# A chunked recurrence cut into pieces: hand-placed half steps with a fixed order on each engine, in place of a scheduler's order

## The chip, the cores and the metric

The kernel runs on one core of a Trainium2 chip. The metric is the device time of one execution in microseconds (us); three runs of the kernel before have a median of 3324.03 us (3309.18 to 3331.33). Names: PE is TensorE, DVE VectorE, ACT ScalarE, POOL GpSimd, SP SyncE, on whose queue the transfers stand.

## What is computed

Three layers of a transformer-like model run one after another in one launch. The change touches the middle one, whose mixer is a recurrence over 256 context positions and 512 positions of the sequence, for 16 heads of 64 channels, once forwards and once backwards:

```python
def step(S, inp):                       # S: 64 x 64 state of one head
    w_t, k_t, v_t, kk_t, kka_t = inp[:5]
    S = (S * w_t[:, :, None, :]
         - jnp.einsum('bhij,bhj->bhi', S, kk_t)[..., None] * kka_t[:, :, None, :]
         + v_t[..., None] * k_t[:, :, None, :])
    y = jnp.einsum('bhij,bhj->bhi', S, inp[5]) if emit else None
    return S, y
...
for d, reverse in enumerate((False, True)):
    s_ctx, y_c = wkv_scan(s0, decay_c, k_dc, v_c, kk_c, a_c, r_c, reverse)
    _, y_d = wkv_scan(s_ctx, decay, k_d, v, kk, a, r, reverse)
    ys.append(y_d)
y = rwkv_readout(ys[0] + ys[1], r, ..., v, g, r_k, ln_g, ln_b, wo, h.dtype)
```

The readout normalises y by head, adds a bonus (the sum over r, k and a weight, times v), multiplies by the gate g and by the matrix wo.

## The kernel before

The recurrence (`class Scan`) works on eight blocks of two heads, 128 channels on the partitions. A block holds both directions, and each direction is cut into 12 chunks of 64 positions (4 of context, 8 of the sequence), so that 24 chunk matrices belong to a block.

`front(blk)` makes what a block needs before its recurrence. It loads keys, decays and rates; for each direction it takes a running sum of the decays on VectorE (L328), exponentials on ScalarE (L330, L331), an affine map (L335), and products on VectorE: `ta` (L337), the key product (L340), the bonus product (L342) and the two parts of `bk` (L344, L345). Then come, for each group g of four chunks, the Gram matrices on TensorE (L362), a mask on VectorE (L365), transposes of `bk` on TensorE (L373), and copies on ScalarE into `tw` (L375) and into `Ld` (L379), which holds the 32x32 blocks on the diagonals.

`rest()` solves and runs the block. The triangular solve transposes `Ld` into `M` (L406, VectorE), does 30 steps of two operations each on GpSimd (L411 multiplies, L412 adds; each step depends on the one before), and transposes back twice on VectorE (L416, L417). The fold puts the solved 32x32 blocks together to 64x64 matrices `T` and multiplies them into the Gram parts: copies L421, matmuls L429 and L438 with copies L433 and L441, matmuls L451 with copies L453 (`FX`). The chain is the sequential part, 12 steps:

- TensorE makes `u` from V and the state Z (L467, L485), ScalarE copies it to X (L488);
- TensorE makes `z` (L473, L492, L495), VectorE scales it to the next Z (L498);
- TensorE adds to Y (L503, L504).

The readout follows: squares, sums by head, a reciprocal root on VectorE of nine tiny operations (L595 to L599), a broadcast (L607, L611), the product of v and bonus on GpSimd (L523), and three operations on VectorE (L525, L526, L530).

The program calls `front` and `rest` block by block. Which instruction of one block goes ahead of which of another, on each engine, is decided by a scheduler that orders the traced program ahead of time; each engine then takes its own row strictly in order. `front` of a block may overlap `rest` of the block before it, as two sets of tiles (`hp`) exist. In the last block 192 instructions of the output matmul (L1270) are tied to steps of the chain by `interleave`. PSUM has three buffers of tag `a` (Gram parts, transposes), one each of `f`, `z` and `y`, and two of `u`.

Of the kernel before, what the change touches and what calls it, by code (L numbers as in the profile page):

```python
# [10 lines left out]
F32 = mybir.dt.float32  # L11
# [13 lines left out]
CH = 64  # L25
# [200 lines left out]

class Scan:

# [3 lines left out]
    def __init__(self, prog):  # L232
# [6 lines left out]
        self.fp = self.pool("sc_f", 1, "right")  # L239
# [5 lines left out]
        self.P, self.Ld = {}, {}  # L245
# [41 lines left out]
    def interleave(self, work, steps, first=0):  # L287

        for k, i in enumerate(work):
            g = steps[first + k * (len(steps) - first) // len(work)]  # L290
            self.p.tc.add_manual_dep(i, g.name, mybir.DependencyInfo(mybir.DependencyClass.NoSync, mybir.DependencyReason.DATA), reason="interleave")
# [9 lines left out]
    def front(self, blk):  # L301
# [16 lines left out]
        order = (lambda t: ((slice(0, NT), t),),
                 lambda t: ((slice(0, NC_), t[:, NC_ - 1::-1]), (slice(NC_, NT), t[:, :NC_ - 1:-1])))

        brk = hp.tile([128, 128], F32, name="brk")
        nc.gpsimd.tensor_scalar(brk, self.bdiag, self.p.col("rk", blk), None, ALU.mult)
        bon = self.p.pt("a")
        TW, A = [], []
        for d in range(2):
            s, ta = load("sg", NT, self.p.sd[blk, d]), load("ta", NT, self.p.td[blk, d])
            cs = fp.tile([128, NT], F32, name="cs", tag="cs")
            nc.vector.tensor_tensor_scan(cs, self.mreset, s, 0.0, ALU.mult, ALU.add)  # L328

# [24 lines left out]
            tw = [hp.tile([128, 8 if i else 4, 2, 3 if i else 2, CH], F32, name=f"tw{d}{i}") for i in range(2)]
            side = lambda h, c: bk[dr[h], c, h:h + 2, :].rearrange("p a t -> p (a t)")
            for g in range(3):
                na, t = (2, tw[1][:, g * 4 - 4:g * 4]) if g else (1, tw[0])
                pss = [self.p.pt("a")[:, :4 * na * CH].rearrange("p (c a t) -> p c a t", c=4, a=na) for h in range(2)]
                for c in range(4):
                    for h in range(2):  # L360
                        rhs = al[dr[h], (g - 1) * 4 + c] if g else ac[dr[h], c]
                        nc.tensor.matmul(pss[h][:, c], side(h, g * 4 + c), rhs.rearrange("p a t -> p (a t)"), start=True, stop=True)  # L362
                for h in range(2):
                    mask = self.mscan.rearrange("p (a t) -> p a t", a=2)[:, :na].unsqueeze(1).to_broadcast([128, 4, na, CH])
                    nc.vector.tensor_tensor(t[:, :, h, :na, :], pss[h], mask, ALU.mult)  # L365
                if g == 1:
                    continue

                n, c0 = (8, 4) if g else (4, 0)
                pts = [self.p.pt("a") for h in range(2)]  # L370
                for c in range(n):
# [1551 lines left out]
```

## Time and profile before

| | |
|---|---|
| median of the three runs | 3324.03 us |
| profiled execution: time, span | 3327.71, 3325.9 us |
| mean granted TensorE clock | 0.884 of full speed |
| busy share of the span: PE, DVE, ACT, POOL | 87%, 49%, 44%, 32% |
| first `M` transpose (L406) to last | 1323.1 to 1987.7 us |
| last Y matmul of the recurrence (L504) starts | 2133.7 us |

The recurrence lies between about 1390 and 2134 us of the span. Busy shares are means over the whole program; what lies in the stretch of the recurrence is read from windows and timelines of it alone. The granted clock of TensorE is given as a share of 2.4 GHz, so 0.50 is 1.2 GHz.

### The profile page before, as it was taken

The page shows a single profiled execution, that of the slowest core. Times are in us where ns is not written, and L with a number is a line of the kernel's source. Part 1 is how long each engine was busy: PE and PEld are TensorE (multiplying, and loading weights), DVE is VectorE, ACT ScalarE, POOL GpSimd, SP SyncE. Part 2 cuts the span into 40 slices and gives each one's busy share as a digit, 9 for nine tenths or more (in the row PEclk, how much of TensorE's full clock was granted, in tenths as well). Part 3 has the DMA queues.
Part 4 walks back from the last instruction along what each step waited for, and adds up shares of the span by engine and source line. Part 5 has one row for each costly group of instructions (what it writes and reads, how often), then busy time and mean ns, then how long its engine had stood idle before and what let it go on. Part 6 is the DMA issues. An engine that isn't in the chain of part 4 may idle for free.

```text
span 3325.9 us, 53211 instructions
## 1 busy us (share of the span) xinstructions
PE 2894.5 (87%) x21242; PEld 2431.2 (73%) x21242; DVE 1627.1 (49%) x3063; ACT 1471.5 (44%) x2849; POOL 1054.1 (32%) x1437
## 2 busy tenths in 40 slices
PE   6998989999996999867667765879999799999999
PEld 6966878888884888656556654667778596578887
DVE  7566364444458446342343431164444575555354
ACT  3257566666655534323333331255553435534342
POOL 4014545677654000343333223025551320020000
PEclk9989989999997899866666667889999896999999
DMA  5423223333313523411112112225542121022322
GB/s 213 139 72 101 93 73 115 124 127 125 126 55 130 193 107 133 120 54 25 39 46 52 52 25 84 83 68 178 174 166 100 57 79 45 1 76 85 105 92 87
DMA packets 125048, 317.55 MB, mean 95 GB/s; under 512 B 36480, under 2 KB 44416, under 8 KB 107776
## 3 DMA queue, kind: packets, MB, share of 16 engines
q1 hardware_dynamic: 124800, 314.15, 28.0%
q8 instruction: 167, 2.74, 0.3%
q14 instruction: 81, 0.66, 0.1%
HBM read 275.57 MB, written 38.54 MB: 94 GB/s over the span
## 4 chain that ended last, share of the span: by engine, by line
PE 30%; POOL 8%; ACT 5%; DMA 4%; DVE 4%; issue 2%; SPq 0%; POOLq 0%; ACTq 0%; DVEq 0%
PE mm L574 6%; PE mm L575 6%; PE mm L576 6%; DMA adaw<-in_ada_dram 3%; POOL acc L717 3%; POOL M L412 2%; POOL Mt L411 2%; PE a L362 2%; ACT wh L567 1%; PE a L1270 1%; PE st L1231 1%; ACT adat L716 1%; PE a L1890 1%; PE b L1225 1%; PE a L1893 1%
## 5 line engine op out<-in xcount | busy, mean ns | idle before, releaser
L717 POOL TENSOR_TENSOR acc<-acc,adat 128x256 f32<-128x256 f32 x658 | 575.4, 896 | 543.2 <-ACT acc L713 436.9
L568 DVE TENSOR_TENSOR wl<-wr,wh 128x2048 fp32r<-128x2048 f32 (+3 forms) x145 | 314.6, 2169 | 382.6 <-ACT wh L567 374.8
L716 ACT ACTIVATE adat<-adaw,silu 128x256 f32<-128x256 f32 x644 | 319.8, 508 | 265.0 <-POOL acc L717 169.5
L567 ACT CAST wh<-wr 128x2048 fp32r<-128x2048 f32 (+2 forms) x147 | 264.8, 1801 | 239.8 <-PE mm L575 217.2
L574 PE MATMUL mm<-fh,wh 128*128 128x512 f32 (+1 forms) x1008 | 349.3, 354 | 19.3 <-DVE relu L999 13.2
L575 PE MATMUL mm<-fl,wh 128*128 128x512 f32 (+1 forms) x1008 | 351.8, 351 | 2.6 <-DVE fl L581 2.6
L576 PE MATMUL mm<-fh,wl 128*128 128x512 f32 (+1 forms) x1008 | 351.0, 350 | 1.0 <-DVE wl L568 1.0
L574 PE MATMUL mm<-h_xhi,wh 128*128 128x512 f32 (+1 forms) x784 | 277.6, 359 | 2.7 <-ACT h_xhi L580 2.7
L575 PE MATMUL mm<-h_xlo,wh 128*128 128x512 f32 (+1 forms) x784 | 277.5, 357 | 0.3 <-DVE h_xlo L581 0.3
L576 PE MATMUL mm<-h_xhi,wl 128*128 128x512 f32 (+1 forms) x784 | 277.5, 356 | 0.0
L574 PEld LDWEIGHTS mm<-fh,wh 128*128 128x128 f32 x1008 | 191.0, 190 | 48.2 <-DVE relu L999 15.6
L648 POOL TENSOR_TENSOR acc<-acc,t 128x256 f32<-128x256 f32 x127 | 108.7, 863 | 350.7 <-ACT t L646 347.9
L575 PEld LDWEIGHTS mm<-fl,wh 128*128 128x128 f32 x1008 | 191.6, 190 | 29.1 <-DVE fl L581 5.7
L576 PEld LDWEIGHTS mm<-fh,wl 128*128 128x128 f32 x1008 | 191.3, 190 | 25.8 <-DVE wl L568 1.2
L411 POOL TENSOR_TENSOR Mt<-M 128x30 f32<-128x30 f32 (+14 forms) x240 | 116.9, 487 | 240.2 <-DVE M L406 133.4
L1023 DVE TENSOR_TENSOR y<-mm,y 128x512 f32<-128x512 f32 (+1 forms) x184 | 99.2, 559 | 143.4 <-PE mm L576 142.7
L574 PE MATMUL mm<-h_hi,wh 128*128 128x512 f32 (+1 forms) x408 | 160.7, 398 | 7.2 <-ACT h_hi L669 7.2
L576 PEld LDWEIGHTS mm<-h_xhi,wl 128*128 128x128 f32 x784 | 148.7, 190 | 21.3 <-issue 0.2
L574 PEld LDWEIGHTS mm<-h_xhi,wh 128*128 128x128 f32 x784 | 147.5, 190 | 22.3 <-ACT h_xhi L580 3.0
L575 PEld LDWEIGHTS mm<-h_xlo,wh 128*128 128x128 f32 x784 | 148.7, 191 | 19.3 <-DVE h_xlo L581 0.7
L575 PE MATMUL mm<-h_lo,wh 128*128 128x512 f32 (+1 forms) x408 | 159.9, 393 | 0.0
L473 PE MATMUL z<-V,tw 64*64 64x64 f32 x704 | 46.2, 254 | 130.3 <-DVE Z L498 128.0
(450 smaller groups left out, 7048.0 us busy)
## 6 DMA issues: line engine op xcount, KB each, us to landing
adaw<-in_ada_dram SPq DMA_DIRECT2D x256, 256.0 KB, 2.7
wr<-in_w_dram SPq DMA_DIRECT2D x64, 1024.0 KB, 4.9
wr<-in_wup_dram SPq DMA_DIRECT2D x22, 1024.0 KB, 4.8
wr<-in_wdn_dram SPq DMA_DIRECT2D x16, 704.0 KB, 4.0
wr<-in_win_dram SPq DMA_DIRECT2D x9, 1024.0 KB, 4.9
wr<-in_evin_dram SPq DMA_DIRECT2D x8, 1024.0 KB, 4.8
sd<-lr_out SPq DMA_DIRECT2D x16, 384.0 KB, 2.6
td<-lr_out SPq DMA_DIRECT2D x16, 384.0 KB, 2.3
```

The costliest lines, as they stand in the source:

```text
L362: nc.tensor.matmul(pss[h][:, c], side(h, g * 4 + c), rhs.rearrange("p a t -> p (a t)"), start=True, stop=True)
L411: nc.gpsimd.tensor_tensor(t, a, b, ALU.mult)
L412: nc.gpsimd.tensor_tensor(M[:, s + 1:, :s], M[:, s + 1:, :s], t, ALU.add)
L567: nc.scalar.copy(hi[:, :n], raw[:, :n])
L568: (eng or nc.vector).tensor_tensor(lo[:, :n], raw[:, :n], hi[:, :n], ALU.subtract)
L574: mm(out, lhs[0], rhs[0], start=first, stop=False)
L575: mm(out, lhs[0], rhs[1], start=False, stop=False)
L576: return mm(out, lhs[1], rhs[0], start=False, stop=last)
L648: nc.gpsimd.tensor_tensor(acc, acc, sq, ALU.add)
L716: nc.scalar.activation(t, w, AF.Copy, scale=s)
L717: nc.gpsimd.tensor_tensor(acc, acc, t, ALU.add)
L1023: nc.vector.tensor_tensor(yb, ps[:, :n], yb, ALU.add)
```

## The change

`front` and `rest` are cut into lists of pieces: `elements` (loads, and for each direction decay, keys and bonus), `grams` (six pieces, one for each direction and group), `solve` (five: first transpose; steps 1 to 10 on VectorE; 11 to 20 on GpSimd; 21 to 30 on VectorE; back-transposes), `fold` (11 pieces), `values` (loads of V by group) and `readout` (three). `chain` becomes a generator that stops after each half step, so 24 times. `slot(blk)` walks the chain of one block and issues, behind the half steps named in its tables, the end of the fold of the same block, the solve and fold of the next block, the elements and Gram pieces of the one after, and the readout of the one before. `pin` then ties each instruction on TensorE, VectorE, ScalarE and GpSimd to the one traced before it on the same engine, so that the traced order stands; SP's queue is not tied. `interleave` is gone: the output matmuls are 32 parts of three at half steps 2 to 23 of the last slot.

The key product and the bonus product move from VectorE to GpSimd; 20 of 30 solve steps move from GpSimd to VectorE. The decay tile P is kept once for each direction rather than for each parity, with a small copy PC of its chunk ends; `al` and `tw` are tiles by group, with a third set for the last group; some element tiles have two sets; V has one set of tiles by group. Loads of the output matrix can start when the chain of block 6 ends.

```diff
+    def solve(self, blk):
...
+                eng.tensor_tensor(t, a, c, ALU.mult)
+                eng.tensor_tensor(M[:, s + 1:, :s], M[:, s + 1:, :s], t, ALU.add)
...
-                nc.vector.tensor_tensor(f[:, c], f[:, c], v3(t), ALU.mult)
+                    nc.gpsimd.tensor_tensor(f[:, c], f[:, c], v3(t), ALU.mult)
...
-            nc.vector.tensor_tensor(v3(pr), v3(r if d == 0 else r[:, ::-1]), f[:, NPC:], ALU.mult)
+                nc.gpsimd.tensor_tensor(v3(pr), v3(r if d == 0 else r[:, ::-1]), f[:, NPC:], ALU.mult)
...
+            if p + 1 < NP:
+                U = begin(p + 1)
+            yield
...
+    def slot(self, blk, work=()):
...
+        put(self.fold(blk)[9:], (0, 1))
+        if blk + 1 < 8:
+            put(self.solve(blk + 1), (0, 1, 2, 9, 10))
+            put(self.fold(blk + 1)[:9], (11, 12, 13, 14, 15, 16, 19, 20, 23))
+            put([lambda: self.values(blk + 1, 0), lambda: self.values(blk + 1, 1)], (8, 16))
+        if blk:
+            put([lambda: self.values(blk, 2)], (0,))
+        if blk > 0:
+            put(self.readout(blk - 1), (3, 5, 6))
+        if blk + 2 < 8:
+            put(self.elements(blk + 2), (0, 2, 4, 8, 7, 10, 12))
+            put(self.grams(blk + 2), (13, 14, 17, 18, 21, 22))
...
+        for k, _ in enumerate(self.chain(blk)):
+            for f in at.pop(k, ()):
+                f()
...
-        scan.rest()
-        for blk in range(1, 7):
-            scan.front(blk)
-            scan.rest()
-        scan.front(7)
...
+        for f in scan.elements(1) + fold[:9] + scan.grams(1):
+            f()
+        for blk in range(7):
+            scan.slot(blk)
```

VectorE's row in a block in the middle, before: from the transpose that opens the solve to the first operation of the next block (Z is the chain's state, P the decays, Dd and Ld the solved blocks, ac a Gram operand).

```order
L406 STREAM_TRANSPOSE M<-Ld_13843 128x1024
L498 TENSOR_TENSOR Z<-z,P_12755 128x128 x7
L416 STREAM_TRANSPOSE Ld_13843<-M 128x32x32
L417 STREAM_TRANSPOSE Dd<-M 128x32x32
L498 TENSOR_TENSOR Z<-z,P_12755 128x128 x4
L351 SCALAR_TENSOR_TENSOR ac_17072<-kkin,P_12755 128x256
```

Seven of a block's eleven Z operations stand ahead of the back-transposes, which need the end of the block's own solve, and four behind.

VectorE's row in a slot in the middle, now, with the lines of the changed kernel: from the end of the ten solve steps behind Z0 (L457, L458) over the elements (scan L357, ta L365, bk L376, the copy L366) to Z2 (the three L584) and the first of the readout's nine tiny operations (L621, L732 and on).

```order
L457 TENSOR_TENSOR Mt<-M 128x210
L458 TENSOR_TENSOR M<-M,Mt 128x21x10
L357 SCALAR_TENSOR_TENSOR cs<-mreset,sg 128x768
L365 SCALAR_TENSOR_TENSOR ta<-ta,kkin 128x768
L366 COPY PC<-P_12755 128x12
L584 TENSOR_TENSOR Z<-z,PC 128x128
L621 TENSOR_SCALAR gnv<-f 128x8
L376 TENSOR_TENSOR bk<-ta,cs 128x12x64
L584 TENSOR_TENSOR Z<-z,PC 128x128
L732 TENSOR_SCALAR rs_r<-gnv 128x8
```

A little further in the same row the readout's end stands ahead of Z3, and the second direction's elements ahead of Z4.

```order
L744 COPY rb<-rs_r 128x512
L633 SCALAR_TENSOR_TENSOR ysb<-ysb,cols,f 128x512
L634 SCALAR_TENSOR_TENSOR ysb<-ysb,cols,sq 128x512
L635 TENSOR_TENSOR ysb<-ysb,rb 128x512
L584 TENSOR_TENSOR Z<-z,PC 128x128
L357 SCALAR_TENSOR_TENSOR cs<-mreset,sg 128x768
L365 SCALAR_TENSOR_TENSOR ta<-ta,kkin 128x256
L365 SCALAR_TENSOR_TENSOR ta<-ta,kkin 128x512
L366 COPY PC<-P_12757 128x12
L386 TENSOR_TENSOR bk<-bk,cs 128x12x64
L584 TENSOR_TENSOR Z<-z,PC 128x128
```

The Z operations, which stood alone before, now have solve steps, elements and readout between them, at fixed places.

GpSimd's row in the same slot, now: the last of the ten solve steps, then the readout's product (L623, which writes the sq that L634 above reads), then the key and bonus products (L375, L380).

```order
L457 TENSOR_TENSOR Mt<-M 128x220
L458 TENSOR_TENSOR M<-M,Mt 128x11x20
L623 TENSOR_TENSOR sq<-sq,vb 128x512
L375 TENSOR_TENSOR bk<-bk,kin 128x12x64
L380 TENSOR_TENSOR prod<-rin,bk 128x512
L375 TENSOR_TENSOR bk<-bk,kin 128x4x64
L375 TENSOR_TENSOR bk<-bk,kin 128x8x64
L380 TENSOR_TENSOR prod<-rin,bk 128x512
```

Before, this row held all 60 solve operations of a block in one run and no key or bonus products.

TensorE's row at a pair of Gram pieces, now (L427 Gram matrices and L435 transposes of two pieces; L559, L570, L574, L553 the chain's half step between them; L582 the next one).

```order
L427 MATMUL a<-al,bk 128x128 x8
L435 MATMUL a<-cst,bk 128x64 x8
L559 MATMUL z<-V,tw 64x64 x4
L570 MATMUL u<-Z,al 64x64 x4
L574 MATMUL z<-Z,cst 128x128
L553 MATMUL u<-V,tw 64x64 x4
L427 MATMUL a<-al,bk 128x128 x8
L435 MATMUL a<-cst,bk 128x64 x8
L582 MATMUL z<-X,FX 64x64 x4
```

Before, Gram pieces and fold matmuls stood together with no step of a chain between them; one such float matmul of the order is two instructions of the trace.

## Rows read from the trace of the kernel before

**Rows 1.** Windows: start and end, length, busy us (instructions) of PE, PEld, DVE, ACT, POOL; clock.

```profile
1670.00:1764.00 94.00, 62.25 (x1002) 54.13 (x1002) 35.06 (x60) 29.96 (x64) 32.05 (x63) 0.65 0.18 46
```

**Rows 2.** Instructions of line L406: durations in ns, minimum, median, maximum; first and last start.

```profile
L406 DVE STREAM_TRANSPOSE M<-Ld x8: 1935/1974/2067, 1323.1 to 1987.7; 128x1024 f32<-128x1024 f32 x8
```

**Rows 3.** Timeline of DVE: start, duration (us), instruction, count, idle before and its releaser.

```profile
1721.66 0.29 DVE L498 TENSOR_TENSOR Z<-z,P 128x128 f32<-128x128 f32 x1 [1.62 <-PE z L495]
1741.30 1.91 DVE L416 STREAM_TRANSPOSE Ld<-M 128x1024 f32<-128x1024 f32 x1 [19.35 <-POOL M L412]
```

**Rows 4.** Windows of 3 us in the stage of Gram matrices and fold.

```profile
1679.00:1682.00 3.00, 2.77 (x15) 2.55 (x16) 1.17 (x3) 1.22 (x4) 0.32 (x1) 0.50 0.28 107
...
1682.00:1685.00 3.00, 3.00 (x23) 3.00 (x21) 3.00 (x5) 0.33 (x1) 0.00 (x0) 0.50 0.36 93
...
1703.00:1706.00 3.00, 3.00 (x46) 2.47 (x42) 1.89 (x2) 2.56 (x7) 0.00 (x0) 0.59 0.00 0
1706.00:1709.00 3.00, 2.60 (x48) 1.99 (x48) 0.82 (x2) 1.17 (x3) 1.83 (x7) 1.00 0.41 131
```

**Rows 5.** Timeline of POOL, the solve's steps 1, 11 and 21.

```profile
1706.70 0.25 POOL L411 TENSOR_TENSOR Mt<-M 128x30 f32<-128x30 f32 x1 [27.39 <-PE a L343]
...
1717.13 0.59 POOL L411 TENSOR_TENSOR Mt<-M 128x220 f32<-128x220 f32 x1
...
1731.20 0.55 POOL L411 TENSOR_TENSOR Mt<-M 128x210 f32<-128x210 f32 x1
```

**Rows 6.** Timelines of DVE and POOL where both work.

```profile
1452.93 1.37 DVE L345 TENSOR_TENSOR bk<-bk,cs 128x768 f32<-128x768 f32 x1
...
1452.19 1.29 POOL L411 TENSOR_TENSOR Mt<-M 128x240 f32<-128x240 f32 x1
...
1771.63 0.17 DVE L599 SCALAR_TENSOR_TENSOR rs_r<-rs_t,rs_r 128x8 f32<-128x8 f32 x1
1771.83 1.24 DVE L597 SCALAR_TENSOR_TENSOR rs_t<-rs_r 128x8 f32<-128x8 f32 x1
```

**Rows 7.** Groups by form, 1389.8 to 2135 us: count, busy us, mean ns, idle before.

```profile
L365 DVE TENSOR_TENSOR tw<-a,c_mscan 128x512 f32<-128x512 f32 x56 | 37.2, 686 | 42.1 <-PE a L362 41.9
L328 DVE TENSOR_TENSOR_SCAN cs<-mreset,sg 128x768 f32<-128x768 bf16 x13 | 22.8, 1755 | 11.1 <-DMA sg<-sd 11.1
L379 ACT COPY Ld<-tw 32x128 f32<-32x128 f32 x56 | 16.5, 294 | 25.1 <-DVE tw L365 23.9
L344 DVE TENSOR_TENSOR bk<-ta,cs 128x768 f32<-128x768 f32 x13 | 12.4, 954 | 2.7 <-ACT cs L331 2.7
L335 ACT ACTIVATE bk<-ta,be,al 128x768 f32<-128x768 f32 x12 | 12.3, 1027 | 16.2 <-DMA ta<-td 16.1
L330 ACT ACTIVATE P<-cs 128x768 f32<-128x768 f32 x13 | 10.9, 838 | 17.0 <-DVE cs L328 9.7 <-DVE Z L498 7.4
L375 ACT COPY tw<-a 128x256 f32<-128x256 f32 x28 | 10.0, 373 | 7.0 <-PE a L373 5.9 <-PE a L362 0.3
L523 POOL TENSOR_TENSOR sq<-sq,vb 128x512 f32<-128x512 f32 x7 | 10.0, 1422 | 183.8 <-DMA ta<-td 61.6 <-DMA sq<-vd 56.3 <-issue 34.8
```

**Rows 8.** Timeline of PE at 1.2 GHz: Gram, fold and transposes.

```profile
1681.62 3.74 PE L362 MATMUL a<-al,bk 64*128 64x128 f32 x23
...
1693.48 1.49 PE L429 MATMUL f<-Dd,tw 32*32 32x32 f32 x48
1694.90 0.69 PE L373 MATMUL a<-cst,bk 64*128 64x64 f32 x8
...
1702.45 1.97 PE L451 MATMUL f<-tw,T 64*64 64x64 f32 x32
```

**Rows 9.** Timeline of ACT: the last copy of the values.

```profile
1387.66 0.59 ACT L1525 COPY vblk<-v 128x512 f32<-128x512 f32 x1 [1.82 <-PE v L1522]
```

**Rows 10.** Timeline of DVE in the last block's chain.

```profile
2097.30 0.29 DVE L498 TENSOR_TENSOR Z<-z,P 128x128 f32<-128x128 f32 x1 [5.72 <-PE z L495]
```

**Rows 11.** Instructions of line L504 on PE, columns as in rows 2.

```profile
L504 PE MATMUL y<-FX,X x512: 217/218/366, 1437.6 to 2133.7; 64*64 64x64 f32 x171
```

**Rows 12.** DMA issues of the page: count, KB each, us to landing.

```profile
sd<-lr_out SPq DMA_DIRECT2D x16, 384.0 KB, 2.6
```

More of the change, by code (lines that the diff above doesn't have):

```diff
@@ L243, in __init__ @@
         nc.vector.memset(self.mreset[:, ::CH], 0.0)
-        self.P, self.Ld = {}, {}
+        self.P = []
+        for d in range(2):
+            P = self.cp.tile([128, NT // CH, 1 + CH], F32, name=f"P{d}")
+            nc.vector.memset(P[:, :, 0:1], 1.0)
+            self.P.append(P)
+        self.Ld = {}
         self.fixed(0)
@@ L285, in late, with pin @@
             nc.gpsimd.memset(self.T[q * 32:q * 32 + 32, :, 32:64], 0.0)
[L287 to L291, printed above, removed]
+        cur = nc.cur_bb
+        self.mark = len(cur.bb.instructions)
+    def pin(self):
+        traced = self.nc.cur_bb.bb.instructions
+        last = {}
+        for i in traced[self.mark:]:
+            if str(i.engine) not in PINNED:
+                continue
+            if i.engine in last:
+                self.p.tc.add_manual_dep(i, last[i.engine], mybir.DependencyInfo(mybir.DependencyClass.NoSync, mybir.DependencyReason.DATA),
+                                         reason="order")
+            last[i.engine] = i.name
     def drop(self, q):
@@ L365, in front @@
[L365 to L371, printed above, removed]
+                    mask = self.mscan.rearrange("p (a t) -> p a t", a=2)[:, :na[g]].unsqueeze(1).to_broadcast([128, 4, na[g], CH])
+                    nc.vector.tensor_tensor(tw[:, :, h, :na[g], :], pss[h], mask, ALU.mult)
@@ L509, in rest, with finish @@
+    def finish(self, blk):
+        b = self.B[blk]
+        y = b["y"] = self.tmp.tile([128, NX], F32, name="ysb", tag="ysb", bufs=1)
+        self.nc.scalar.copy(y, b["Y"])
         if blk == 0:
             self.p.tap("ysum0", y)
[L511 to L515 removed]
@@ new lines, in slot, with put @@
+    def slot(self, blk, work=()):
+        at = {}
+        def put(pieces, places):
+            for f, k in zip(pieces, places, strict=True):
+                at.setdefault(k, []).append(f)
+        put(self.fold(blk)[9:], (0, 1))
[10 more added lines that the diff above has]
+            put(self.grams(blk + 2), (13, 14, 17, 18, 21, 22))
+        for k, f in work:
+            at.setdefault(k, []).append(f)
+        for k, _ in enumerate(self.chain(blk)):
+            for f in at.pop(k, ()):
+                f()
+        assert not at
+        self.finish(blk)
@@ L1246, in layer1 @@
         scan.late()
-        scan.rest()
-        for blk in range(1, 7):
-            scan.front(blk)
-            scan.rest()
-        scan.front(7)
-        scan.drop(scan.fp)
+        fold = scan.fold(0)
+        for g in range(3):
+            scan.values(0, g)
+        for f in scan.elements(1) + fold[:9] + scan.grams(1):
+            f()
+        for blk in range(7):
+            scan.slot(blk)
+        scan.drop(scan.fp[0])
         scan.drop(scan.hp[0])
@@ L1536, in features @@
         scan = Scan(self)
-        scan.front(0)
+        for f in scan.elements(0) + scan.grams(0) + scan.solve(0):
+            f()
         values(wv)
```

402 lines of the change are left out of this document (234 added, 168 removed).

## The prediction

> **What bounds the kernel now.** I read the windows by block first, then the timelines of VectorE and GpSimd inside one block, then the TensorE clock in short windows, then the groups by form for prices.
>
> In the block from 1670 to 1764 us no engine is full: TensorE 62 of 94 us at a mean granted clock of 0.65, VectorE 35, ScalarE 30, GpSimd 32 [rows 1]. The eight transposes that open the triangular solve start from 1323.1 to 1987.7 [rows 2]: (1987.7-1323.1)/7 = 94.9 us a block. So a block is bound by waits, and there are two.
>
> First, the chain. A step at 2.4 GHz takes 1.62 us of waiting plus 0.29 = 1.91 us [rows 3]. Seven steps run beside GpSimd's solve; then VectorE's row has the back-transpose (L416) ahead of the eighth Z, and VectorE sits idle 19.35 us until GpSimd ends the solve [rows 3]. From the end of the last Z (1721.66+0.29) to the end of the two transposes (1741.30+1.91, and another such) the chain stands still for some 23 us.
>
> Second, the stage after it, where the next block's Gram matrices and the fold follow each other on TensorE. There the granted clock is 0.50 (1.2 GHz) with TensorE full, from the window at 1679 on, and 2.4 GHz is back only in the window at 1706 [rows 4].
>
> **The change part by part.** Nearly all arithmetic stays; the order decides. I follow one slot from its Z0 to the next slot's Z0 along the in-order rows of the engines.
>
> *What is removed.* No Z stands behind a back-transpose of the block that is about to be folded: the solve is now a block ahead. That frees the 23 us. What takes their place must be walked.
>
> *Z0 to Z3.* Behind Z0 VectorE has ten solve steps, 20 small dependent operations, which the trace has only on GpSimd: there they take 1717.13-1706.70 = 10.4 us [rows 5], the upper bound. The lower one is the 0.20 us from start to start of two tiny dependent operations [rows 6], 20x0.20 = 4.0. With sizes around that of the Z operation (128 columns, 0.29 us [rows 3]) plus a gap I take 6.5. Then GpSimd does steps 11 to 20: 1731.20-1717.13 = 14.1 us [rows 5]. Behind them on its row stands the readout's product with vb, 1.42 [rows 7]; VectorE's L634 (a line of the changed kernel, the second operation of the readout's end) waits for that product, and L635 and Z3 are queued behind L634, and TensorE's next step behind Z3. L634 and L635 cost about 0.69 each (128x512, as L365 [rows 7]), Z 0.29: 6.5+14.1+1.4+1.4+0.3 = 23.7. So the wait for GpSimd comes back, shorter, through the readout.
>
> To this comes what VectorE holds up. Where VectorE's two-input operations met solve operations, they took turns: L345 took 1.37 where L344, of the same size, takes 0.95, and the solve operation beside it 1.29 where another of nearly its size takes 0.59 [rows 5 to 7]. In the 14 us VectorE runs the scan, 1.76, ta and bk, 0.95 each [rows 7], and the readout's nine small ones, some 1 us: 4.7. With it 28.4. Bounds: 4.0+14.1+1.4+1.7 = 21.2 (GpSimd loses nothing) and 10.4+14.1+4.7+1.4+1.7 = 32.3.
>
> The Trainium skill, page "SBUF — State Buffer", section "SBUF: two separate sides", goes further: a VectorE instruction with two SBUF inputs and a GpSimd one that reads SBUF exclude each other for a whole instruction. By that rule each of the nine small operations would wait for a solve operation, and a block would be some 4.5 us longer than by the row. The trace agrees for the long operations and for one tiny one, 1.24 us [rows 6].
>
> *Z3 to Z4.* The second direction's elements: scan 1.76, two exponentials 0.84 each and the affine 1.03 on ScalarE, then ta and bk on VectorE, 0.95 each, Z 0.29 [rows 3, 7]: 6.7. The key products moved to GpSimd: it shows 1.42 at 128x512 [rows 7], so 2.1 at 768 columns; VectorE's 0.95 is the lower bound. They come before bk and take turns with VectorE's own; I take 8 (6.7 to 9.3).
>
> *Z4 to Z5.* The last ten solve steps on VectorE, sizes mirrored, 6.5 again (4.0 to 10.4), two back-transposes of 1.91 [rows 3], bk 0.95, Z 0.29, a small memset: 11.7. With GpSimd's key products beside them 12 (9.2 to 15.6).
>
> *Z5 to Z6.* One step, and bk behind its GpSimd product: 4 (3 to 5). Z0 to Z6 together 28.4+8+12+4 = 52.4. TensorE has little to do in it.
>
> *Z6 to the next Z0.* Three pairs of Gram pieces, one piece at a half step. A piece at 1.2 GHz is 16 instructions at 3.74/23 = 0.163 (2.6 us) and 16 of the transposes at 0.69/8 (1.38) [rows 8]. Tag a has three buffers, so transposes wait for the mask (0.69 [rows 7]), the second piece for the first copy (0.37), and the next Z stands behind both pieces; al costs 0.84 (two operations of 256 columns), z and Z 0.8: 0.84+2x(2.6+0.69+1.38)+0.37+0.8 = 11.3, plus the second piece's copies ahead of the next X (2x0.37+4x0.294 = 1.9 [rows 7]) = 13.2. At 2.4 GHz the matmuls halve: 9.2. Two chain steps without Grams 7.6 or 3.8. Fold: four pieces of 1.49 and five of 1.97 [rows 8], 15.8, or 7.9. In all 63.0 at 1.2 GHz and 39.3 at 2.4. Before, a full TensorE got its clock back after 1706-1679 = 27 us [rows 4]; with 25 us slow, 25/63.0 = 0.40 of the work is done, and the rest fast makes 25+0.60x39.3 = 48.6; I take 50.
>
> So a slot is T = 52.4+50 = 102.4 us against 94.9.
>
> *Ends.* The blocks' values end at 1387.66+0.59 [rows 9]; only then do the pools for elements(1) exist. Per direction scan, three ScalarE operations, three VectorE ones and the key products are about 10 us, 20 for both; 4 of the fold not hidden beside them; three Gram pairs 40 at the slow clock: Z0 of slot 0 at 1388+20+4+40 = 1452. Slot 0 lacks a readout, 8 us less. Slot 6 has no elements and Grams: 23.7+2+11+3 up to Z6 and 26 for five steps and the fold = 66. Slot 7 keeps the output matmuls: twelve steps at 5.72+0.29 = 6.0 [rows 10] and 2 to start: 74. The last Y comes at 1452-8+66+74+6T = 1584+6T = 2198. Before it starts at 2133.7 [rows 11], so 2134, and all behind it is unchanged: +64 us. On the profiled execution's own 3327.7 (span 3325.9) that is 3392; it lies 3.7 above the median shown, so by the median 3388. I say 3390. The sign turns at T = (2134-1584)/6 = 91.7.
>
> Costed at nothing: PC's copies of 12 columns (0.17 as the tiny operations [rows 6], twice a slot), brk on GpSimd (ahead of a whole slot), and the loads: V in groups and the elements' are issued half a slot or more ahead of their readers; without that cover each would show its 2.6 us [rows 12].
>
> **The rivals.** *Warm TensorE* (the other side): the chain steps and fold pieces between the Gram pieces keep the clock at 2.4 GHz from Z6 on. For it: the clock is 1.00 in the window at 1706, where chain and fold mix and TensorE is not even full. Against: the windows before it stayed at 0.50 with TensorE full [rows 4], and Z0 to Z6 leaves TensorE mostly idle. The stage is then 39.3 us, or 2x(1.3+0.69)+1.9 = 5.9 a pair and 29.4 in all if masks and copies hide as well: T = 82 to 92, last Y 2075 to 2134, 3265 to 3324. It decides from a stage of 39.3 us downwards.
>
> *Free port.* VectorE's operations don't hold GpSimd, and its solve steps run at their lower bound: T = 102.4-4.7-2x2.5 = 92.7, 3330, as before. Against it the turns of rows 6.
>
> *Cold TensorE.* The stage is at 1.2 GHz throughout: T = 52.4+63.0 = 115.4, +142, 3466. For it the 27 full microseconds at 0.50 [rows 4].
>
> *Full exclusion.* Each of the nine small operations waits for a solve operation, as one did: 9x0.5 = 4.5 us more, T = 106.9, +91, 3415. Against it: the one before it took 0.17 [rows 6]. The Trainium skill's page "SBUF — State Buffer" has this as its rule.
>
> That the change doesn't do what it says (a Z still behind the transposes that wait for GpSimd's whole solve) the order excludes; only its price is open.
>
> **How the numbers follow.** My forecast, T from 95 to 109: 0.38, 3345 to 3430. Warm TensorE 0.30, two thirds of it under 3291. Free port 0.10. Warm and free together 0.05 (T about 77, 3236). Cold 0.10. Full exclusion 0.07. A difference under 1% (33 us) can't be told from none here. Faster by over 1%: 0.20+0.05 = 0.25. Within 1% (3291 to 3357): a third of warm 0.10, free port 0.10, the edge of the forecast 0.02 = 0.22. Slower: the rest, 0.53. The range 3265 to 3475 leaves out warm and free together and the far ends of warm and cold, 0.15 to 0.2.
>
> **What would show it.** In the changed profile VectorE should wait some 10 us for GpSimd's product ahead of L634, with Z3 behind it; Z0 to Z3 near 28, the ten steps on VectorE near 6.5; the starts of the solve's transposes 102 apart (under 92: wrong in the sign); the clock 0.50 in the first 20 us or so behind Z6, and Gram pairs 13 apart there. If Z0 of slot 0 is far from 1452 or slot 7 far from 74, the ends are wrong. If L634 waits for nothing, the first wait was misread; if Z0 to Z6 is near 52 and the rest under 40, the clock was.

## The result, and the profile after

The changed kernel takes 3369.48 us (median of four runs, 3368.12 to 3381.77) against 3322.76 of the kernel before in the same comparison. The ratio of the means is 1.0153, 95% interval 1.0111 to 1.0195, so 1.5% slower. Forecast were 3390 us, slower by over 1% with a chance of 0.53, and a range of 3265 to 3475. In the profiled execution the span grew from 3325.9 to 3368.5 us, and the last Y matmul of the recurrence starts at 2178.7 instead of 2133.7 [rows 11]: the 45 us lie in the recurrence. Lines in this part are those of the changed kernel: Z is L584, the solve's first transpose L463, the readout's end L633 to L635.

The first view answers to rows 2 and 11: the solve's eight transposes, and the last line of the chain (durations in ns, minimum, median, maximum; first and last start).

```profile
L463 DVE STREAM_TRANSPOSE M<-Ld x8: 1959/1978/2003, 1332.3 to 2023.9; 128x1024 f32<-128x1024 f32 x8
...
L595 PE MATMUL y<-FX,X x512: 217/310/312, 1482.5 to 2178.7; 64*64 64x64 f32 x171
```

The median of the Y matmul rose from 218 [rows 11] to 310 ns: the chain now runs mostly at the slow clock (0.50, so 1.2 GHz). The second view cuts slot 2 into the five parts of the prediction (columns as in rows 1), Z0 to Z3, to Z4, to Z5, to Z6, and to the next Z0; the last line is the whole slot.

```profile
1634.96:1664.00 29.04, 11.75 (x189) 10.18 (x183) 19.39 (x44) 5.24 (x9) 20.03 (x23) 0.67 0.20 55
1664.00:1672.13 8.13, 6.11 (x52) 3.89 (x52) 5.43 (x7) 2.75 (x4) 3.37 (x3) 0.50 0.26 83
1672.13:1684.30 12.17, 3.44 (x50) 2.91 (x50) 11.48 (x27) 0.27 (x1) 1.21 (x1) 0.50 0.10 33
1684.30:1689.44 5.14, 4.77 (x40) 2.81 (x41) 1.18 (x3) 4.88 (x7) 0.58 (x1) 0.51 0.28 80
1689.44:1733.22 43.78, 38.90 (x708) 34.44 (x708) 13.35 (x28) 18.98 (x56) 0.02 (x1) 0.69 0.11 29
1634.96:1733.22 98.26, 64.98 (x1035) 54.23 (x1031) 50.83 (x104) 32.11 (x76) 25.21 (x27) 0.64 0.16 44
```

VectorE's busy time in a block rose from 35 us [rows 1] to 51, in a slot that is longer, not shorter. The third view is VectorE's timeline in slot 2, with the waits inside Z0 to Z4.

```profile
1634.96 0.26 DVE L584 TENSOR_TENSOR Z<-z,PC 128x128 f32<-128x128 f32 x1
1635.13 0.21 DVE L457 TENSOR_TENSOR Mt<-M 128x30 f32<-128x30 f32 x1
...
1641.66 1.75 DVE L357 TENSOR_TENSOR_SCAN cs<-mreset,sg 128x768 f32<-128x768 bf16 x1
1646.12 1.30 DVE L365 SCALAR_TENSOR_TENSOR ta<-ta,kkin 128x768 f32<-128x768 f32 x1 [2.70 <-ACT bk L363]
...
1657.18 0.75 DVE L633 SCALAR_TENSOR_TENSOR ysb<-ysb,cols,f 128x512 f32<-128x512 f32 x1 [2.24 <-PE f L748]
1660.13 2.27 DVE L634 SCALAR_TENSOR_TENSOR ysb<-ysb,cols,sq 128x512 f32<-128x512 f32 x1 [2.20 <-POOL sq L623]
1662.44 1.63 DVE L635 TENSOR_TENSOR ysb<-ysb,rb 128x512 f32<-128x512 f32 x1
1664.00 0.28 DVE L584 TENSOR_TENSOR Z<-z,PC 128x128 f32<-128x128 f32 x1
```

The ten solve steps take 1641.66-1635.13 = 6.5 us. L634 does wait for GpSimd's product, with Z3 behind it, but only 2.2 us and not 10. Ahead of it lies a wait for ScalarE of 2.70 us that the prediction's sum for this part doesn't have.

The table gives, from each kernel's one profiled execution, the parts for the slots 1 to 5 in us (means; from the starts of the Z operations) and the stage from Z6 to the next Z0 for the slots 0 to 5 one by one; the ratios are of the means over its executions. Runs below are named as in the experiments.

| kernel | ratio to before (95%) | Z0-3 | Z3-4 | Z4-5 | Z5-6 | Z6 to next Z0, slots 0 to 5 |
|---|---|---|---|---|---|---|
| forecast | 1.020 | 28.4 | 8 | 12 | 4 | 50 each |
| changed | 1.0153 (1.0111-1.0195) | 29.0 | 8.1 | 12.2 | 5.1 | 47.2 33.8 43.8 40.5 44.3 44.4 |
| e1 product first | 1.0054 (1.0032-1.0077) | 27.4 | 9.0 | 12.2 | 5.1 | 33.8 44.2 45.8 44.4 33.8 40.5 |
| e2 all VectorE | 1.0298 (1.0280-1.0316) | 36.1 | 8.1 | 12.2 | 5.1 | 44.4 44.4 44.3 44.4 44.3 44.2 |
| e3 affine first | 1.0015 (0.9985-1.0046) | 28.8 | 5.1 | 12.2 | 5.1 | 33.8 33.8 43.8 40.5 44.2 44.3 |
| e4 e1 and e3 | 1.0008 (0.9986-1.0031) | 23.5 | 9.7 | 12.1 | 5.1 | 33.8 40.5 45.8 44.4 45.8 44.3 |
| e5 only TensorE's row kept | 1.0010 (0.9992-1.0027) | 16.9 | 9.3 | 7.1 | 4.9 | 51.8 57.2 55.7 50.4 49.5 52.0 |
| e6 keys on VectorE | not settled | 27.3 | 6.5 | 12.9 | 4.8 | 33.8 six times |
| e7 all GpSimd | 1.0185 (1.0147-1.0222) | 32.7 | 7.3 | 9.6 | 5.1 | 44.4 44.3 44.3 44.2 44.2 44.2 |
| e8 24 fillers | 1.0136 (1.0069-1.0202) | 29.0 | 8.1 | 12.3 | 5.1 | 44.4 six times |
| e9 44 fillers | 0.9991 (0.9970-1.0012) | 29.0 | 8.1 | 14.2 | 3.2 | 41.2 41.2 41.2 33.8 33.8 33.8 |
| e10 three edits | 0.9984 (0.9964-1.0005) | 25.0 | 4.9 | 12.8 | 5.2 | 33.8 43.8 44.2 40.5 44.2 44.2 |
| e11 three and 44 fillers | 0.9872 (0.9851-0.9894) | 24.7 | 4.9 | 15.5 | 3.2 | 33.8 33.8 33.8 33.7 33.8 33.8 |

The last column is the first thing to see: the same instructions take 33.8 us in some slots and 40 to 47 in others, of one execution. Windows of 3 us show why. Slot 1 of the changed kernel (Z6 at 1601.20):

```profile
1598.00:1601.00 3.00, 3.00 (x20) 1.32 (x20) 0.00 (x0) 2.91 (x5) 0.14 (x1) 0.57 0.27 98
1601.00:1604.00 3.00, 2.86 (x87) 2.61 (x82) 0.79 (x3) 1.53 (x3) 0.46 (x1) 1.00 0.00 0
...
1625.00:1628.00 3.00, 1.92 (x31) 1.53 (x31) 1.75 (x5) 0.10 (x1) 0.00 (x0) 1.00 0.38 83
```

and slot 2 (Z6 at 1689.44):

```profile
1688.00:1691.00 3.00, 3.00 (x75) 2.21 (x74) 0.62 (x2) 1.52 (x3) 0.60 (x1) 0.78 0.02 5
1691.00:1694.00 3.00, 2.54 (x45) 2.17 (x42) 1.09 (x3) 1.78 (x5) 0.00 (x0) 0.79 0.00 0
1694.00:1697.00 3.00, 3.00 (x62) 2.59 (x64) 0.00 (x0) 1.58 (x6) 0.00 (x0) 0.50 0.30 69
...
1718.00:1721.00 3.00, 3.00 (x67) 2.93 (x65) 0.29 (x1) 1.48 (x6) 0.00 (x0) 0.66 0.00 0
1721.00:1724.00 3.00, 2.65 (x54) 2.39 (x56) 0.96 (x3) 1.05 (x3) 0.00 (x0) 1.00 0.12 27
```

In both the clock rises around Z6. In slot 1 it stays at 1.00, through a window in which TensorE is busy only 1.92 of 3 us. In slot 2 it falls back to 0.50 within two windows, with TensorE busy 2.5 to 3 of 3 us, and is 1.00 again only some 27 us later, though TensorE is nearly always busy. Whole stages, the slots 0, 1, 3, 4 and 5 (slot 2 is the fifth line of the second view; the clock stands third from the end):

```profile
1499.86:1547.04 47.18, 42.35 (x707) 37.60 (x708) 13.35 (x28) 18.98 (x56) 0.02 (x1) 0.62 0.10 27
1601.20:1634.96 33.76, 28.63 (x706) 25.21 (x707) 13.35 (x28) 19.25 (x56) 0.26 (x1) 1.00 0.14 38
1787.70:1828.19 40.49, 35.56 (x708) 31.56 (x708) 13.35 (x29) 18.97 (x56) 0.01 (x1) 0.78 0.11 31
1882.63:1926.98 44.35, 39.48 (x707) 35.02 (x708) 13.33 (x28) 18.98 (x56) 0.02 (x1) 0.68 0.06 14
1981.44:2025.82 44.38, 39.55 (x707) 35.01 (x708) 13.35 (x29) 18.98 (x56) 0.00 (x0) 0.68 0.06 14
```

Since the clock is either 0.50 or 1.00, a stage with the mean c spent the share 2*(1-c) of its length at 0.50: some 36, 27, 18, 28 and 28 us in the slots 0, 2, 3, 4 and 5, and nothing in slot 1. No stage was at 0.50 throughout.

### The profile page after: what moved, and what is told of

It reads as the page before. It is cut to its first block, busy times and chain, and to the rows that moved or that the text cites. A ratio compares the mean times of both kernels' runs of the same rounds, so it can differ in the third digit from the quotient of the medians.

```text
span 3368.5 us, 53407 instructions
## 1 busy us (share of the span) xinstructions
PE 2898.9 (86%) x21242; PEld 2422.3 (72%) x21242; DVE 1740.0 (52%) x3399; ACT 1485.5 (44%) x2945; POOL 990.1 (29%) x1149
## 4 chain that ended last, share of the span: by engine, by line
PE 37%; DVE 8%; POOL 6%; ACT 4%; issue 3%; DMA 2%; SPq 0%; POOLq 0%; ACTq 0%; DVEq 0%
PE mm L711 7%; PE mm L712 7%; PE mm L713 7%; PE a L427 2%; POOL acc L854 2%; DMA adaw<-in_ada_dram 2%; POOL M L458 2%; POOL Mt L457 2%; DVE Mt L457 1%; ACT wh L704 1%; DVE M L458 1%; PE st L1368 1%; PE a L1410 1%; DVE tw L430 1%; PE a L2038 1%
## 5 line engine op out<-in xcount | busy, mean ns | idle before, releaser
L711 PE MATMUL mm<-fh,wh 128*128 128x512 f32 (+1 forms) x1008 | 349.7, 355 | 17.1 <-DVE relu L1136 12.2
L457 POOL TENSOR_TENSOR Mt<-M 128x220 f32<-128x220 f32 (+4 forms) x80 | 57.4, 717 | 401.2 <-DVE M L458 395.6
L713 PE MATMUL mm<-h_hi,wl 128*128 128x512 f32 (+1 forms) x408 | 159.3, 393 | 0.0
```

What stands on the lines that cost most here:

```text
L457: eng.tensor_tensor(t, a, c, ALU.mult)
L711: mm(out, lhs[0], rhs[0], start=first, stop=False)
L713: return mm(out, lhs[1], rhs[0], start=False, stop=last)
```

## The experiments

All but the last start from the changed kernel. Since the clock shifts a stage by 10 us, a part is judged by its own length in the table, and the whole time by the ratio. Theory A said that GpSimd's row decides Z0 to Z3, through the readout's product; theory B that VectorE's own row with its waits for ScalarE does.

**e1, the product ahead of the solve steps.**

```diff
-            put(self.readout(blk - 1), (3, 5, 6))
+            put(self.readout(blk - 1), (1, 5, 6))
```

> The readout's first piece moves from half step 3 to half step 1, so that GpSimd's product sq x vb stands ahead of the ten solve steps on its row. Theory A (GpSimd's row decides Z3, through the product behind the steps): the idle 2.2 us ahead of L634 and the stretching of L634 and L635 (2.27 and 1.63 us) go, Z0 to Z3 falls from 29.0 to 25 or 26 us; 3.5 us in each of slots 1 to 5 and 5 in slot 6, about 22 us less than the changed kernel: 3347. Theory B (VectorE's own row with its waits for ScalarE decides): another wait stands there at once, under 1 us a slot, 3365 to 3370.

Z0 to Z3 fell by 1.6 us and Z3 to Z4 rose by 0.9. The wait for the product is gone, and others stand in its place (VectorE's timeline, one slot):

```profile
1652.30 0.75 DVE L633 SCALAR_TENSOR_TENSOR ysb<-ysb,cols,f 128x512 f32<-128x512 f32 x1 [2.17 <-PE f L748]
1653.16 0.75 DVE L634 SCALAR_TENSOR_TENSOR ysb<-ysb,cols,sq 128x512 f32<-128x512 f32 x1
1654.99 1.74 DVE L635 TENSOR_TENSOR ysb<-ysb,rb 128x512 f32<-128x512 f32 x1 [1.07 <-DMA rb<-gd]
1656.65 0.28 DVE L584 TENSOR_TENSOR Z<-z,PC 128x128 f32<-128x128 f32 x1
```

So 0.8 us a slot net, as theory B has it. The ratio fell more than that; in the profiled execution two of the six last stages were short instead of one, which is 11 us that the edit can't be given.

**e2, all solve steps on VectorE.**

```diff
-... lambda: steps(nc.gpsimd, range(11, 21)), last, back]
+... lambda: steps(nc.vector, range(11, 21)), last, back]
```

> Solve steps 11 to 20 run on VectorE too. Theory A: nothing on GpSimd is left to wait for, Z0 to Z3 falls from 29 to 24 us or less, 30 us or more off: under 3340. Theory B: VectorE gets 20 operations of about 0.4 us, 8 us, in the row of the chain, and loses the turns with GpSimd: Z0 to Z3 at 30 to 31, Z3 to Z4 and Z4 to Z5 1 us shorter each; 3360 to 3380, the same.

Both theories missed: Z0 to Z3 grew by 7.1 us, and nothing behind it got shorter. Theory A's 24 us fall: VectorE no longer waits for GpSimd ahead of Z3, and its own row alone takes 36 us. The 20 operations cost VectorE nearly their whole length, while on GpSimd they had lain beside VectorE's other work and its waits.

**e3, the affine map ahead of the exponentials on ScalarE.**

```diff
+                nc.scalar.activation(bk[:, :, 1, :], v3(ta), AF.Identity, ...)
                 nc.scalar.activation(P[d][:, :, 1:], v3(cs), AF.Exp, scale=-C0)
                 nc.scalar.activation(cs, cs, AF.Exp, scale=C0)
-                nc.scalar.activation(bk[:, :, 1, :], v3(ta), AF.Identity, ...)
```

> ScalarE does the affine map, on which VectorE's ta waits (2.70 us idle, twice a slot), ahead of the two exponentials. Theory A: Z0 to Z3 stays at 29, as GpSimd ends no earlier; only Z3 to Z4 falls from 8.1 to 5.4: 16 us less, 3353. Theory B: both waits go, 5.4 us a slot, 32 us less, 3337.

Z3 to Z4 fell by 3.0 us, Z0 to Z3 by 0.2, as theory A has it: with VectorE early, GpSimd's product is what Z3 waits for (idle ahead of L634 2.93 instead of 2.20 us). So each theory is right where the other's wait is taken away: two paths to Z3 are within 2 us of each other. The ratio lies 46 us below that of the changed kernel, where 3.2 us a slot make 16 (two of the ten executions, of 3361.62 and 3361.78 us, are left out of it). The last stages were 14 us shorter in the profiled execution, which the edit can't be given; the rest is not accounted for.

**e4, both.**

> The product ahead of the solve steps and the affine map first, together. If both waits in the stretch Z0 to Z3 stand in for each other (A and B both hold, each covers part of the other): Z0 to Z3 22 us, Z3 to Z4 5.4, so 9.7 us a slot, 58 us less than the changed kernel, 3311, more than the two alone add up to. If they are independent, the sum of the two runs alone: 3331 by theory A's sizes.

Z0 to Z3 fell to 23.5 us, by 5.5 where the two alone gave 1.6 and 0.2: they do stand in for each other. But Z3 to Z4 grew to 9.7, where VectorE's product of bk waits 1.35 us for GpSimd's bonus product, which now comes too late. Net 3.9 us a slot, not 9.7, which with slot 6 makes some 23 us; the ratio lies 48 below that of the changed kernel, and this rest, too, is not accounted for.

**e5, only TensorE's row kept.**

```diff
-PINNED = ("EngineType.PE", "EngineType.DVE", "EngineType.Activation", "EngineType.Pool")
+PINNED = ("EngineType.PE",)
```

> Only TensorE's row keeps the traced order; VectorE, ScalarE and GpSimd get the scheduler's order, in which the scan and small solve steps stand between the Z operations in another mix. If the hand-made order of these three rows costs time (theory: Z0 to Z6 is the sum of what is traced ahead of each Z), Z0 to Z6 falls from 54.4 to 46 or so: 50 us less than the changed kernel, 3320. If the sum of work and the TensorE row decide, within 10 us of 3369.

Z0 to Z6 fell to 38.3 us, further than the 46 expected. But the stage behind grew to 50 to 57 us, since scans, ta and bk that the hand-made order keeps ahead of Z6 now stand among the Gram masks. A slot is 91 instead of 96 us, and the whole ratio 1.0010, the time of the kernel before. So the order of these three rows costs 1.4%.

**e6, keys and bonus on VectorE.**

```diff
-                    nc.gpsimd.tensor_tensor(f[:, c], f[:, c], v3(t), ALU.mult)
+                    nc.vector.tensor_tensor(f[:, c], f[:, c], v3(t), ALU.mult)
...
-                nc.gpsimd.tensor_tensor(v3(pr), ...)
+                nc.vector.tensor_tensor(v3(pr), ...)
```

> The key and bonus products are back on VectorE, as before. Theory B (VectorE's own row is the bound from Z0 to Z6): 3.3 us of products come into the row, some 2 us of taking turns with GpSimd go: 1 to 2 us a slot longer, 3375 to 3385. Theory A (GpSimd's products are waited for): 2 to 3 us a slot shorter, 3350 to 3357.

Z0 to Z6 fell by 2.9 us: theory A's size. Turns with GpSimd cost more than the products: L634 and L635, which took 2.27 and 1.63 us beside GpSimd's products, take 0.75 and 0.69. The whole time doesn't answer: the four executions took 3282.15, 3295.7, 3350.13 and 3360.79 us, at mean granted clocks of 0.901, 0.898, 0.879 and 0.877. The two shorter ones alone give a ratio of 0.9897 (0.9848 to 0.9945), the two longer ones lie some 1% above the kernel before. The profiled one (3295.7) had all six last stages at 33.8, without any filler.

**e7, all solve steps on GpSimd.**

> All 30 solve steps run on GpSimd, in the same three pieces at the same places. Theory B alone (VectorE's row): 13 us go from it, Z0 to Z6 falls from 54.4 to 42, 70 us less, 3300. With GpSimd's chain of 35 us (10.4+14.1+10.4) and its products behind each other, Z3 at 32, Z5 at 52, Z6 at 55 behind Z0: no change, 3365 to 3380. Together with the run in which all steps are on VectorE this says on which engine the solve is cheaper.

Z0 to Z6 is 54.8 us instead of 54.4. Theory B alone fails; the sum along GpSimd's row held (Z3 at 32.7 for 32). The timeline has the wait that the prediction looked for: VectorE is idle for 12.78 us ahead of L634 until GpSimd's product ends. So the split in the change is better than all steps on VectorE (e2); from all on GpSimd it can't be told apart, as the intervals of the two ratios overlap.

**e8, 24 fillers.** A filler is a matmul whose result nobody reads.

```diff
+        def warm(n):
+            def go():
+                ps = self.p.pt("a")
+                i = self.p.cst("ident")
+                for _ in range(n):
+                    self.nc.tensor.matmul(ps[:, :128], i, i, start=True, stop=True)
+            return go
+        if blk < 6:
+            put([warm(24)], (10,))
```

> Behind half step 10 of slots 0 to 5 TensorE does 24 extra 128x128x128 matmuls whose result nobody reads, while VectorE does the last ten solve steps and TensorE would be idle. Theory W (the granted clock decides the stage from Z6 to the next Z0: 33.8 us in the one slot of the changed kernel whose clock was 1.00 throughout, 40 to 47 in the five others): all six stages come to about 34, 50 us less, 3320. Rival (masks, copies and the chain bound the stage, the clock only goes along): 3369 to 3380, with the fillers' own 2 us a slot where they end behind VectorE's steps.

All six stages at 44.4 in the profiled execution, so by its expectation theory W falls. Its windows ahead of Z5 (at 1690.5) show more:

```profile
1683.00:1686.00 3.00, 3.00 (x28) 3.00 (x27) 2.62 (x13) 0.00 (x0) 0.00 (x0) 0.94 0.00 0
1686.00:1689.00 3.00, 2.62 (x38) 2.36 (x36) 3.00 (x2) 0.00 (x0) 0.00 (x0) 1.00 0.00 0
1689.00:1692.00 3.00, 1.18 (x18) 1.04 (x18) 2.63 (x4) 1.38 (x2) 0.00 (x0) 0.70 0.14 13
1692.00:1695.00 3.00, 3.00 (x14) 1.17 (x14) 0.00 (x0) 2.93 (x5) 0.00 (x0) 0.50 0.33 123
...
1722.00:1725.00 3.00, 2.32 (x23) 1.96 (x21) 0.82 (x2) 0.25 (x1) 0.00 (x0) 0.61 0.00 0
```

The fillers raised the clock to 1.00, ended too early, and it fell in the window in which TensorE was busy 1.18 of 3 us. It stayed at 0.50 for some 33 us.

**e9, 44 fillers.**

```diff
+            put([warm(44)], (10,))
```

> As the run with 24 fillers behind half step 10, with 44, so that TensorE is busy from Z4's step until Z5 arrives. With 24 the clock rose to 1.00 early and fell again at a gap of some 2 us ahead of Z5, and all six stages stayed at 44.4. Theory W (it fell because of that gap): with no gap the clock stays up, six stages of 34, 50 us less than the changed kernel, 3320. Rival (the fall does not hang on that gap): stages at 44 as before, and where the fillers run slow they end behind VectorE's steps, up to 7 us a slot: 3375 to 3410.

The ratio fell from 1.0153 to 0.9991, though TensorE has 264 matmuls more and Z5 comes 2 us later. In the profiled execution, the slowest of its ten (3306.69 to 3338.92), three stages are 33.8 and three 41.2. In one of these (Z6 at 1688.0) the fall comes later than in e8:

```profile
1692.00:1695.00 3.00, 2.94 (x75) 2.47 (x75) 0.26 (x1) 2.59 (x8) 0.00 (x0) 1.00 0.25 58
1695.00:1698.00 3.00, 2.82 (x60) 2.60 (x61) 0.79 (x3) 1.83 (x6) 0.00 (x0) 0.67 0.17 35
1698.00:1701.00 3.00, 3.00 (x66) 2.48 (x64) 0.00 (x0) 1.21 (x3) 0.00 (x0) 0.50 0.04 8
```

So theory W holds for the time, but not in its cause: here the clock fell with TensorE busy 2.8 to 3 of 3 us, and TensorE had not been idle for more than 0.5 us at a time since 1672. Nor is it shown that the fillers work by keeping TensorE busy: e6 had six short stages without them.

**e10, three edits (e1, e3, e6).**

> Three edits together: product ahead of the solve steps, affine map first, key and bonus products back on VectorE. If VectorE's own row with its waits for ScalarE is what Z0 to Z6 hangs on: 27.3-2.7 to Z3, 6.5-2.7 to Z4, 12.9, 4.9, so 46 us instead of 54.4, 8 a slot, 48 us less at the same clocks: 3320; with all six later stages at the fast clock 3270, with all slow 3335. If GpSimd is still waited for, Z0 to Z6 stays above 50 and the time above 3340.

Z0 to Z6 is 47.9 us instead of 54.4, where 46 was expected; the time, 3318.07 us for 3320 expected, is that of the kernel before within 0.2%.

**e11, the three edits and 44 fillers.**

> The three edits and the 44 fillers. Theory W: 46+34 = 80 us a slot in every execution, 3270 or less with little spread, faster than the kernel before by over 1%. Rival: stages at 44, 3335 and above.

3282.53 us (3274.06 to 3294.06), 1.3% faster than the kernel before and 2.8% than the changed one; a slot takes 82 us where 80 was expected. All five executions lie below the twelve of e10, which has the same edits without fillers (3305.49 to 3333.45). In the profiled one all six stages are 33.8; one of them as a window:

```profile
1652.68:1686.43 33.75, 28.61 (x706) 25.18 (x707) 13.34 (x29) 19.16 (x56) 0.26 (x1) 1.00 0.14 38
```

It has the 708 matmuls of slot 2 above but for two that the trace lacks; TensorE's busy time is 28.6 us for 38.9, and VectorE's and ScalarE's are the same within 0.2 us.

**e12, the kernel before with fillers in its stall.**

```diff
             Z = Zn
+            if p == 7 and blk < 7:
+                ps = self.p.pt("f")
+                for _ in range(90):
+                    fi = nc.tensor.matmul(...)   # tied behind steps[-1]
```

> The kernel before, with 90 extra matmuls on TensorE in blocks 0 to 6 at the place where it stands still for 20 us (behind the z of step 7, while VectorE waits for GpSimd's solve); the order of VectorE's row is as before (seven Z ahead of the back-transposes, four behind). Theory W (TensorE's idle stretch costs the clock of the stage behind it): the steps, the Gram matrices and the fold behind the stall run at 2.4 GHz instead of 27 us at 1.2; 8 to 12 us a block, 50 to 80 us less, 3245 to 3275. Rival (in this kernel the later gaps, where TensorE waits for loads and masks at 1670 to 1679, bring the clock down again whatever stands ahead): within 10 us of 3324.

3449.36 us, a ratio of 1.0386 (1.0358 to 1.0414). The place was missed: the z of step 7 itself waits for ScalarE's X, which comes only behind the stall, so the fillers ran behind it and added their own 22 us a block. Some 4 of these came back in the steps right behind them; the stage from there to the next block's first Z stayed at 46 to 49 us, for 45 to 48 before. They still say something. The clock was 1.00 behind them, fell when TensorE ran out of work for 6.64 us ahead of the Gram matrices, and came back 34 us later:

```profile
1715.00:1718.00 3.00, 3.00 (x63) 2.85 (x60) 2.97 (x3) 0.83 (x1) 0.00 (x0) 1.00 0.86 189
1718.00:1721.00 3.00, 0.53 (x10) 0.39 (x8) 2.09 (x6) 2.55 (x3) 1.01 (x1) 1.00 0.30 86
1721.00:1724.00 3.00, 0.00 (x0) 0.00 (x0) 3.00 (x6) 0.00 (x0) 0.75 (x1) 0.52 0.09 16
...
1754.00:1757.00 3.00, 3.00 (x39) 2.06 (x37) 1.94 (x1) 1.88 (x4) 0.51 (x2) 0.79 0.00 0
```

That is the mechanism of the rival of its expectation, though not its time; whether fillers inside the stall would do more was not tried.

## Why the prediction was right, and where its steps were not

**Prologue.** Z0 of slot 0 was forecast for 1452 and came at 1451.56; its parts were not read one by one.

**Z0 to Z6.** 52.4 us were forecast and 54.4 measured, each part within 1.2 us. The path to Z3 was the one told, ten steps on VectorE, ten on GpSimd, the product, L634, L635, Z3, but two of its terms were off and partly cancel. GpSimd's ten steps, with what VectorE held up, took 17.0 us (1641.92 to 1658.9) where the sum had 14.1+4.7 = 18.8. L634 and L635 took 3.9 us where it had 1.4, as they met the key and bonus products that the change put on GpSimd; without these (e6) they take 1.4.

```profile
1658.83 1.26 POOL L623 TENSOR_TENSOR sq<-sq,vb 128x512 f32<-128x512 f32 x1
1660.06 1.80 POOL L375 TENSOR_TENSOR bk<-bk,kin 128x768 f32<-128x768 f32 x1
```

Two steps inside were not as told. The wait ahead of L634 is 2.2 us and not 10: VectorE's own row, with 2.70 us for ScalarE and 2.24 for TensorE's broadcast, which the sum left out of this part, arrives almost as late (27.4 us in e1, where the product isn't waited for). So "the wait for GpSimd comes back, shorter, through the readout" is true of the row and half true of the time: e1 alone saves 0.8 us, e3 alone 3.2, both 3.9. And PC's two copies, costed at nothing with 0.17 us each, took 0.61 and 1.23 us beside GpSimd's work.

**Z6 to the next Z0.** This is the term that was mis-sized: 50 us were forecast, and the mean of the six slots is 42.3. The picture behind it, some 25 us at 1.2 GHz and the rest at 2.4, is what four of the six slots did (36, 27, 28 and 28 us at 1.2 GHz); one had 18 and one none, so it is no rule. The two sizes were too large. At 2.4 GHz the stage is 33.8 us for 39.3. At 1.2 GHz none ran to its end, but each of the five mixed stages gives an estimate: slot 4 spent 28.4 us at 1.2 GHz and 15.9 at 2.4, in which 15.9/33.8 = 0.47 of the work was done if it is spread evenly, so the whole at 1.2 GHz would be 28.4/0.53 = 54 us. The other four come to 53 to 54 as well, where the sum had 63.0. With 54 and 33.8 the forecast's 25 slow us make 43. The sum put all the fold's pieces behind the Gram pairs and beside no other work; in slot 0 the first two pairs, with fold pieces between them, took 13.0 and 10.9 us where the forecast had 13.2 each and the fold on top.

The rival of a warm TensorE, with a chance of 0.30, came true in slot 1, in e6's profiled execution and in e11's in all six slots; the rival of a cold one in no slot.

**The ends.** Slot 6 took 66.1 for 66. Slot 7 took 2178.7-2091.91 = 86.8 for 74: its second Z waits 17.32 us, because TensorE at the first part of the output matmul, at half step 2, stands idle 9.50 us for loads that are issued from 2089.15 on, only 3 us ahead of that slot's Z0.

```profile
2091.91 0.29 DVE L584 TENSOR_TENSOR Z<-z,PC 128x128 f32<-128x128 f32 x1 [4.58 <-PE z L582]
2103.50 5.46 PE L1410 MATMUL a<-z,wo 128*128 128x256 f32 x12 [9.50 <-DMA z<-zd]
2109.52 0.29 DVE L584 TENSOR_TENSOR Z<-z,PC 128x128 f32<-128x128 f32 x1 [17.32 <-PE z L582]
```

The prediction gave this start 2 us and had no term for these loads.

**The sum.** Against the forecast end of 2198 the six stages are 46 us shorter, Z0 to Z6 is 14 longer (slot 0 lacked 6 us and not 8) and slot 7 is 13 longer, which makes the 2178.7. So the time came out within 20 us partly by luck, as two errors cancel in part.

**The sign.** With the forecast's ends the last Y would have come as early as before if the slots 0 to 5 took 2134-1452-66-74 = 542 us together. They took 574, 32 more, and slot 7 adds the other 13 of the 45 us. The freed stall of 23 us is not lost in one place: the blocks 2 to 5 before took 47.9 us from the start of their first Z (L498) to that of their last, stall included, and 46.4 from there to the next block's first; a slot now takes 54.4 up to Z6, and five steps with the Gram pairs and the fold behind it. With all six last stages at 33.8 the six slots would come to 523 us, an estimate from the table, and the last Y to 2127, as before within 7 us. So slower rather than level hung on how long TensorE's clock stayed at 0.50 behind Z6; the forecast took 25 us of it from the 27 of the kernel before, and four of six slots bore it out. Moving solve steps back is no way out: on GpSimd all thirty gave 54.8 us up to Z6 (e7).

**The other rivals.** Free port: no. L357's scan (1641.66, 1.75 us) and a solve operation of GpSimd met, and that operation took 1.87 us, where the next one of its size took 0.61, and ended 0.4 us behind the scan. Full exclusion of the nine small operations: in part. Five of the nine took 0.46 to 0.55 us and the others 0.17, so about 1.6 us a slot and not 4.5. Two of them, and the solve operation:

```profile
1651.07 0.49 DVE L734 SCALAR_TENSOR_TENSOR rs_t<-rs_r 128x8 f32<-128x8 f32 x1
1651.60 0.17 DVE L735 TENSOR_TENSOR rs_t<-rs_t,gnv 128x8 f32<-128x8 f32 x1
```

```profile
1641.92 1.87 POOL L457 TENSOR_TENSOR Mt<-M 128x220 f32<-128x220 f32 x1 [40.46 <-DVE M L458]
1643.87 0.61 POOL L458 TENSOR_TENSOR M<-M,Mt 128x220 f32<-128x220 f32 x1
```

The Trainium skill, page "SBUF — State Buffer", section "SBUF: two separate sides", has the loser of such a meeting wait out the whole instruction. The trace agrees for the scan; of the small operations four of nine did not wait, such as L735 above, which started between two of GpSimd's solve operations.

## What to carry to other kernels

Walk the in-order row of each engine from one step of the chain to the next; two paths that arrive within a few us of each other must be shortened together, and work that was hidden on another engine costs nearly its whole length in the row that the chain waits for (e2). When small work fills the pauses of a chain, look at what TensorE's clock does behind the pause: here 44 useless matmuls a slot in some 10 us of idleness were worth about as much (1.6%) as anything that was done to the order, though why they help is open. Compare stages of one execution before ratios of whole kernels, because the same code ran in 33.8 and in 44.4 us a slot.

## What was not expected of the hardware

The granted clock of TensorE went back to 0.50 in slot 2 some 4 us after it had risen, while TensorE was busy 85 to 100% of the time, and stayed there for 27 us of almost full work; in e8 it stayed there for some 33 us and in e9 for 20. In other slots with the same instructions it stayed at 1.00, through windows with less work. What decides between the two is open: e8 shows a fall at a gap, e9 a fall without one, e11, with the same 44 fillers and earlier steps, none between Z6 and the next Z0 in its profiled execution, and e6's profiled execution none there with no filler at all. The spread of executions goes with it: e8's four took 3350.75, 3362.4, 3388.9 and 3392.21 us at mean clocks of 0.892, 0.888, 0.875 and 0.872.
